# Changing the layout of the S5 branch's input and output by transfers through DRAM instead of products with the identity

## The chip, the cores and the metric

The kernel runs on one core of one Trainium2 chip. A core has a matrix engine (TensorE, PE in the rows below; its weight loads are listed apart as PEld), VectorE (DVE), ScalarE (ACT), GpSimd (POOL) and SyncE (SP), on whose queue nearly all transfers of this kernel are issued, and 16 DMA engines that move the data. Each engine works through its own instructions in order; what one engine needs of another it waits for on semaphores. The metric is the device time of one execution in microseconds (us).

## The reference

The reference is a two-layer encoder over 256 tokens of width 1024. Each layer normalises its input, projects it (`w_in`), runs three mixers side by side (an mLSTM, a Fourier mixer and an S5 state space), gates and adds them, projects back (`w_out`), and then applies a squared-ReLU MLP. The change concerns the S5 mixer, which works on 256 channels as 16 groups of 16:

```python
u = z_s.reshape(bsz, s, S5_GROUPS, S5_GROUP)
bu_re = einsum('gpc,bsgc->bsgp', bb_re, u)          # and bu_im
_, _, x_re, x_im = lax.associative_scan(combine, (a_re, a_im, bu_re, bu_im), axis=1, reverse=reverse)
y = d_skip * u + s5_direction(u, ..., False) + s5_direction(u, ..., True)
y = jax.nn.gelu(y).reshape(bsz, s, M_S5)
zz = y @ w_glu + b_glu
return zz[..., :D_MODEL] * jax.nn.sigmoid(zz[..., D_MODEL:])
```

## The kernel before

Every large product is computed in split precision. A weight block of 512 KB is loaded into one of five buffers `raw` (L200, on SP's queue), ScalarE rounds it to `whi` (L202), VectorE subtracts to get the rest `wlo` (L204), and TensorE makes three products per block of 128 by 128 (`mm3`: L262 hi by hi, L263 hi by the low part of the activations, L264 lo by hi). `whi` and `wlo` have four buffers each. `wstat_pair` makes 256 columns of a projection this way: 48 products of 256 columns, two weight blocks.

The mixers' smaller steps are Python generators. While the main stream of projections is written out, `tick` lets them emit a few instructions after each weight block. The order in which the instructions then stand on each engine is set when the kernel is built, by a scheduler that lists an instruction where its own model of times has it ready; on the chip this order is fixed.

The S5 branch needs its input in another layout than the projection delivers. The projection leaves `zsT`, in channel layout: partition is one of 128 channels of a half `k`, and the 256 tokens are stored as `(t j)`, four tokens `t` of each of 64 chunks `j` (ScalarE's two instructions of L1024). The state space works on `U`, in chunk layout: partition is `32 t + c` (four tokens by the 32 channels of a pair of groups `g`), and the free axes are eight pairs `g` by 64 chunks `j`. `s5_inputs` makes this with 32 small products per layer: each multiplies 32 columns of the identity (`ident`) by one `t` of one half, and places 32 channels in 32 other partitions of a PSUM bank, `acc_ps(0)`, which ScalarE copies to SBUF (L725). `s5_branch` then makes the input products with `QT` (L737), rotations and scans on VectorE, and the output products ("y products", L768 to L776, all into one PSUM bank `yp`), and the GELU (L781 to L786), which gives `g_`, still in chunk layout. Another 32 products with the identity (L792) bring it to channel layout in PSUM, and ScalarE and VectorE split it into `yg`, the high and the low part (L797, L798, two instructions each). The gated linear unit, `glu_up`, multiplies `yg` by `w_glu`.

In layer 0, `s5_branch` is emitted with the gate projections (its tables are made during the projections before), and `glu_up` follows soon after it. In layer 1 it starts with the projections after `zsT`, and `glu_up` comes some 80 us after `yg`. The mLSTM's cells run in between on the same engines: scores on TensorE (L916), an exponential on ScalarE (L924), a product on VectorE (L925), and the cell's value products on TensorE (L933). At the end, `cell_out` transposes the heads (L188), two per head, through PSUM buffers `acc_ps(0)`, of which there are two, and VectorE reads each (L968).

Of the kernel before, what the change touches and what calls it, by code (L numbers as in the profile page):

```python
# [10 lines left out]
F32 = mybir.dt.float32  # L11
F32R = mybir.dt.float32r
AF = mybir.ActivationFunctionType
# [17 lines left out]
NGP = NG // 2  # L31
# [12 lines left out]
LT = 4  # L44
JN = S // LT
# [73 lines left out]
def encoder_kernel(ctx: ExitStack, tc: tile.TileContext, a: dict, out: bass.AP):  # L119
    nc = tc.nc  # L120
# [9 lines left out]
    dp = ctx.enter_context(tc.tile_pool(name="dp", bufs=2, space=DRAM))  # L130
# [3 lines left out]
    def nm(s):  # L134
        uid[0] += 1
        return f"{s}_{uid[0]}"
# [4 lines left out]
    def acc_ps(which):  # L141
        return accp.tile([P, 512], F32, tag=f"acc{which}", name=nm("acc"))

    def ring(which, shape, dt=F32):
        return bp.tile(shape, dt, tag=f"ring{which}", name=nm(f"ring{which}"))
# [13 lines left out]
    act = nc.scalar.activation  # L159
# [3 lines left out]
    mm = nc.tensor.matmul  # L163
# [6 lines left out]
    ident = cst[:, C_ID:C_ID + P]  # L170
# [177 lines left out]
    def w2k():  # L348
        return sp.tile([P, 512], F32, tag="w2k", name=nm("w2k"), bufs=6)
# [366 lines left out]

    def s5_inputs(zsT):

        up = acc_ps(0)
        for g in range(NGP):  # L720
            for tau in range(LT):
                mm(up[32 * tau:32 * tau + 32, g * JN:(g + 1) * JN], ident[:, 32 * (g % 4):32 * (g % 4) + 32],
                   zsT[:, g // 4, tau, :], start=True, stop=True, skip_group_check=True)
        U = cp.tile([P, NGP, JN], F32, tag="zb2", name=nm("U"))
        act(U, up, AF.Copy)  # L725
        return U

    def s5_branch(l, U, yg):
        Z = ring("A", [P, 2, NGP, 2, JN])
        for d in range(2):  # L730
            plus, minus = (ALU.add, ALU.subtract) if d == 0 else (ALU.subtract, ALU.add)
            for b in range(2):
                g0 = d * NGP + 4 * b
                bps = acc_ps(1)
                for g in range(4):
                    for r in range(2):
                        mm(bps[:, (g * 2 + r) * JN:(g * 2 + r + 1) * JN], QT[:, r, g0 + g, :], U[:, 4 * b + g, :],  # L737
                           start=True, stop=True, skip_group_check=True)
                v4 = lambda t: t.rearrange("p (g r j) -> p g r j", g=4, r=2)
                cb = tabC[:, g0:g0 + 4].unsqueeze(2).broadcast_to([P, 4, 2, JN])  # L740
                sb = tabS[:, g0:g0 + 4].unsqueeze(2).broadcast_to([P, 4, 2, JN])
                zg = Z[:, d, 4 * b:4 * b + 4]
                t1, t2 = v4(w2k()), v4(w2k())
                V.tensor_tensor(t1, v4(bps), cb, ALU.mult)
                V.tensor_tensor(t2, v4(bps), sb, ALU.mult)
                yield 1.2
                V.tensor_tensor(zg[:, :, 0], t1[:, :, 0], t2[:, :, 1], plus)
                V.tensor_tensor(zg[:, :, 1], t1[:, :, 1], t2[:, :, 0], minus)
                for g in range(4):
                    c = l * 2 * NGP + g0 + g  # L750
                    rho = par[:, C_RHO, c:c + 1].broadcast_to([P, JN])
                    for r in range(2):
                        zv = zg[:, g, r, :]
                        if d == 1:
                            zv = zv[:, ::-1]
                        V.tensor_tensor_scan(zv, rho, zv, 0.0, ALU.mult, ALU.add)
                yield 1.8
                t1, t2 = v4(w2k()), v4(w2k())
                V.tensor_tensor(t1, zg, cb, ALU.mult)
                V.tensor_tensor(t2, zg, sb, ALU.mult)  # L760
                yield 1.2
                V.tensor_tensor(zg[:, :, 0], t1[:, :, 0], t2[:, :, 1], minus)
                V.tensor_tensor(zg[:, :, 1], t1[:, :, 1], t2[:, :, 0], plus)
                yield 0.7
        yp = acc_ps(1)
        for g in range(NGP):
            o = g * JN
            mm(yp[:, o:o + JN], Tt[:, g, :], U[:, g, :], start=True, stop=False, skip_group_check=True)  # L768
            for d in range(2):
                for r in range(2):  # L770
                    w = Wt[:, r, d * NGP + g].rearrange("p t c -> p (t c)")
                    if d == 0:
                        mm(yp[:, o + 1:o + JN], w, Z[:, d, g, r, 0:JN - 1], start=False, stop=False,  # L773
                           skip_group_check=True)
                    else:
                        mm(yp[:, o:o + JN - 1], w, Z[:, d, g, r, 1:JN], start=False, stop=r == 1,  # L776
                           skip_group_check=True)
        yield 0.0

        q = w2k()  # L780
        act(q, yp, AF.Square)  # L781
        V.tensor_scalar(q, q, 0.044715, 1.0, ALU.mult, ALU.add)
        V.tensor_tensor(q, yp, q, ALU.mult)
        act(q, q, AF.Tanh, scale=GELU_C)
        g_ = w2k()
        stt(g_, q, 1.0, yp, ALU.add, ALU.mult)  # L786
        yield 1.6
        gp = acc_ps(1)
        for g in range(NGP):
            for t in range(LT):  # L790
                o = ((g // 4) * LT + t) * JN
                mm(gp[32 * (g % 4):32 * (g % 4) + 32, o:o + JN], ident[:, 32 * t:32 * t + 32],  # L792
                   g_[:, g * JN:(g + 1) * JN], start=True, stop=True, skip_group_check=True)
        for ct in range(2):
            src = gp[:, ct * S:(ct + 1) * S].rearrange("p (t j) -> p t j", t=LT)
            tok = lambda t: t.rearrange("p (j t) -> p t j", t=LT)
            act(tok(yg[0][:, ct]), src, AF.Copy, scale=0.5)  # L797
            stt(tok(yg[1][:, ct]), src, 0.5, tok(yg[0][:, ct]).bitcast(F32), ALU.mult, ALU.subtract)  # L798
        yield 0.8
# [186 lines left out]
    def mixer(l, iu, vu, after):  # L986
# [40 lines left out]
        st = {"Gm": ring("B", [P, 8, S])}  # L1027
        fo_y = ring("B", [P, 2, 2, S], F32R)
        U = s5_inputs(zsT)
        if l > 0:  # L1030
            side[1].append(s5_branch(l, U, yg))
# [29 lines left out]
        if l == 0:  # L1061
            side[1].append(s5_branch(l, U, yg))
# [275 lines left out]
```

## Time and profile before

| | us |
|---|---|
| median of 3 runs | 842.99 (841.51 to 843.23) |
| the profiled execution, its own time | 842.77 |
| span of its trace | 841.0 |
| TensorE busy in the span | 822.0 (98%) |
| VectorE busy | 598.3 (71%) |
| ScalarE busy | 473.6 (56%) |
| DMA: moved | 145.80 MB, 173 GB/s in the mean |

The span is what the profiler saw from the first to the last instruction; the execution's own time is 1.77 us longer. Busy times of different engines overlap. A matmul's row in the timeline gives its whole duration, and successive matmuls are pipelined, so TensorE's cost is read from the distance between starts or from the chain of work. A matmul on 32-bit operands that are not rounded stands in the trace as two records, so 32 products with the identity are x64.

### The profile page before, as it was taken

To read this page: it belongs to the slowest core of one execution; us is meant where nothing else is said; L and a number is where in the kernel's file an instruction comes from. 1 tells how busy PE (TensorE), PEld (TensorE's weight loads), DVE (VectorE), ACT (ScalarE), POOL (GpSimd) and SP (SyncE) were. 2 spreads that over 40 slices of the span, in tenths; PEclk is the share of its full clock that TensorE was granted. 3 is DMA by queue.
4 is the path that set the end of the run, shared out by engine and by line. 5 is a ranking of instruction groups with operands and counts; after the bars stand their busy time and mean duration, and the time that the engine had idled before them with its cause. 6 is when DMAs were issued, how large, how long until landed. Compare 5 with 4: busy or idle time off the path is not lost.

```text
span 841.0 us, 15400 instructions
## 1 busy us (share of the span) xinstructions
PE 822.0 (98%) x6081; PEld 760.2 (90%) x6081; DVE 598.3 (71%) x1071; ACT 473.6 (56%) x786; POOL 33.6 (4%) x51
## 2 busy tenths in 40 slices
PE   7999999999989999999999999999999999999996
PEld 5999999999868999999879999999997899999995
DVE  4899889868685577667568798676876855555563
ACT  4669855476464448467654355665855544444451
POOL 1000200010020000000010020000000100000000
PEclk9999999999999999999999999999999999999999
DMA  8765645345845665755836452555556556666651
GB/s 262 224 182 160 215 120 159 116 123 157 271 132 164 187 191 136 240 178 187 270 95 213 139 177 76 151 169 158 176 179 222 177 167 183 192 183 191 186 175 50
DMA packets 116824, 145.80 MB, mean 173 GB/s; under 512 B 17894, under 2 KB 98958, under 8 KB 116496
## 3 DMA queue, kind: packets, MB, share of 16 engines
q1 hardware_dynamic: 116604, 144.56, 56.7%
q8 instruction: 47, 0.77, 0.4%
q10 hardware_dynamic: 148, 0.27, 0.1%
q14 instruction: 25, 0.20, 0.1%
HBM read 143.28 MB, written 1.52 MB: 172 GB/s over the span
## 4 chain that ended last, share of the span: by engine, by line
PE 93%; DVE 2%; ACT 1%; issue 1%; DMA 1%; POOL 1%; SPq 0%; DVEq 0%; POOLq 0%; ACTq 0%
PE mm L262 17%; PE mm L264 17%; PE mm L263 17%; PE acc L263 8%; PE acc L264 8%; PE acc L262 8%; PE mm L279 3%; PE mm L278 3%; PE acc L737 2%; PE mm L295 1%; PE acc L188 1%; PE acc L933 1%; PE mm L281 1%; PE acc L916 1%; PE acc L773 1%
## 5 line engine op out<-in xcount | busy, mean ns | idle before, releaser
L204 DVE TENSOR_TENSOR wlo<-raw,whi 128x1024 fp32r<-128x1024 f32 (+1 forms) x237 | 288.2, 1218 | 157.7 <-ACT whi L202 155.9
L202 ACT ACTIVATE whi<-raw 128x1024 fp32r<-128x1024 f32 (+1 forms) x237 | 248.7, 1051 | 248.6 <-PE mm L263 147.2
L262 PE MATMUL mm<-hT,whi 128*128 128x256 f32 x1024 | 291.3, 284 | 0.0
L264 PE MATMUL mm<-hT,wlo 128*128 128x256 f32 x1024 | 290.7, 284 | 0.0
L263 PE MATMUL mm<-hT,whi 128*128 128x256 f32 x1024 | 290.5, 284 | 0.0
L262 PEld LDWEIGHTS mm<-hT,whi 128*128 128x128 f32 x1024 | 192.7, 188 | 1.7
L263 PEld LDWEIGHTS mm<-hT,whi 128*128 128x128 f32 x1024 | 193.0, 188 | 1.2
L264 PEld LDWEIGHTS mm<-hT,wlo 128*128 128x128 f32 x1024 | 193.2, 189 | 0.3
L263 PE MATMUL acc<-wlo,ringB 128*128 128x512 f32 x280 | 109.3, 391 | 0.7 <-DVE wlo L204 0.7
L264 PE MATMUL acc<-whi,ringB 128*128 128x512 f32 x280 | 108.4, 391 | 0.0
L262 PE MATMUL acc<-whi,ringB 128*128 128x512 f32 x280 | 106.5, 390 | 0.0
L263 PEld LDWEIGHTS acc<-wlo,ringB 128*128 128x128 f32 x280 | 52.6, 188 | 12.1 <-DVE wlo L204 1.9
L264 PEld LDWEIGHTS acc<-whi,ringB 128*128 128x128 f32 x280 | 52.6, 188 | 10.9
L262 PEld LDWEIGHTS acc<-whi,ringB 128*128 128x128 f32 x280 | 52.6, 188 | 10.3
L279 PE MATMUL mm<-whi,hT 128*128 128x512 f32 (+1 forms) x84 | 33.1, 401 | 2.0 <-DVE hT L371 1.8
L278 PE MATMUL mm<-whi,hT 128*128 128x512 f32 (+1 forms) x84 | 32.9, 401 | 0.3 <-ACT hT L370 0.2
L900 DVE SCALAR_TENSOR_TENSOR t1k<-ringB,pc,t1k 128x254 f32<-128x254 f32 (+1 forms) x64 | 31.3, 489 | 0.9
L380 DVE SCALAR_TENSOR_TENSOR w2k<-acc,ringA 128x512 f32<-128x512 f32 x16 | 10.6, 688 | 25.6 <-ACT t1k L378 25.6
L340 POOL TENSOR_SCALAR rs<-ss 128x1 f32<-128x1 f32 x16 | 7.8, 488 | 491.4 <-DVE w2k L380 350.0
L262 PE MATMUL mm<-ringB,whi 128*128 128x256 f32 x96 | 27.3, 286 | 0.0
L263 PE MATMUL mm<-ringB,whi 128*128 128x256 f32 x96 | 27.2, 286 | 0.0
L378 ACT ACTIVATE t1k<-acc 128x512 bf16<-128x512 f32 x16 | 9.5, 595 | 31.4 <-PE acc L264 31.4
(339 smaller groups left out, 1197.9 us busy)
## 6 DMA issues: line engine op xcount, KB each, us to landing
raw<-in_w_ffn_dram SPq DMA_DIRECT2D x128, 512.0 KB
raw<-in_w_in_dram SPq DMA_DIRECT2D x84, 512.0 KB
raw<-in_w_out_dram SPq DMA_DIRECT2D x16, 512.0 KB
raw<-in_w_glu_dram SPq DMA_DIRECT2D x16, 256.0 KB
raw<-in_w_up_mlstm_dram SPq DMA_DIRECT2D x8, 512.0 KB
ringB<-md SPq DMA_DIRECT2D x2, 1024.0 KB
raw<-in_w_up_fourier_dram SPq DMA_DIRECT2D x4, 512.0 KB
raw<-in_w_in_dram SPq DMA_DIRECT2D x4, 408.0 KB
```

Of the source, the lines that this page charges most:

```text
L188: nc.tensor.transpose(o, i, cst[:k, C_ID:C_ID + k])
L202: act(hi, raw, AF.Copy)
L204: latest[0] = V.tensor_sub(lo, raw, hi.bitcast(F32)).ins
L262: mm(o, lhi, rhi, start=start, stop=False)
L263: mm(o, lhi, rlo, start=False, stop=False)
L264: mm(o, llo, rhi, start=False, stop=stop)
L278: mm(o, hhi[:, k, tt], hi, start=k == 0, stop=False)
L279: mm(o, hlo[:, k, tt], hi, start=False, stop=False)
L378: act(junk(), ps[c], AF.Square, accum_out=ss[:, c:c + 1])
L380: stt(f, ps[c], ROOT_D, gpost[:, half(c)], ALU.mult, ALU.mult)
L737: mm(bps[:, (g * 2 + r) * JN:(g * 2 + r + 1) * JN], QT[:, r, g0 + g, :], U[:, 4 * b + g, :], start=True, stop=True, skip_group_check=True)
L900: stt(u[:, lo_:hi_], z[:, lo_ + o:hi_ + o], col(l, "cw", j * 8 + i), u[:, lo_:hi_], ALU.mult, ALU.add)
```

## The change

Both layout changes now go through a scratch tensor in DRAM. On the way in, one transfer writes `zsT` to `zd` (pieces of 256 floats, 1 KB), and four transfers, one for each `t`, read it back to 32 partitions of `U` each (pieces of 64 floats, 256 bytes). On the way out, four transfers write `g_` to `gd` (pieces of 256 bytes), and one reads it back in channel layout to an SBUF tile `gp` (pieces of 1 KB). All ten per layer are issued on SP's queue. The 64 products with the identity per layer and ScalarE's copy to `U` go; the two PSUM tiles go as well; `gp` is now one of the six SBUF tiles `w2k`; and `s5_branch` yields once between the transfers and the reading of `gp`.

```diff
     def s5_inputs(zsT):
 
-        up = acc_ps(0)
-        for g in range(NGP):
-            for tau in range(LT):
-                mm(up[32 * tau:32 * tau + 32, g * JN:(g + 1) * JN], ident[:, 32 * (g % 4):32 * (g % 4) + 32],
-                   zsT[:, g // 4, tau, :], start=True, stop=True, skip_group_check=True)
+        zd = dp.tile([NGP, 32, LT, JN], F32, tag="zd", name=nm("zd"))
+        nc.sync.dma_start(by_channel(zd), zsT.rearrange("p k t j -> p k (t j)"))
         U = cp.tile([P, NGP, JN], F32, tag="zb2", name=nm("U"))
-        act(U, up, AF.Copy)
+        for tau in range(LT):
+            nc.sync.dma_start(U[32 * tau:32 * tau + 32], by_chunk(zd, tau))
         return U
+
+    def by_channel(d):
+
+        return d.rearrange("(k q) c t j -> (q c) k (t j)", k=2)
+
+    def by_chunk(d, tau):
+
+        return d[:, :, tau, :].rearrange("g c j -> c g j")
 
     def s5_branch(l, U, yg):
...
-        gp = acc_ps(1)
-        for g in range(NGP):
-            for t in range(LT):
-                o = ((g // 4) * LT + t) * JN
-                mm(gp[32 * (g % 4):32 * (g % 4) + 32, o:o + JN], ident[:, 32 * t:32 * t + 32],
-                   g_[:, g * JN:(g + 1) * JN], start=True, stop=True, skip_group_check=True)
+        gd = dp.tile([NGP, 32, LT, JN], F32, tag="gd", name=nm("gd"))
+        for t in range(LT):
+            nc.sync.dma_start(by_chunk(gd, t), g_[32 * t:32 * t + 32].rearrange("c (g j) -> c g j", g=NGP))
+        gp = w2k()
+        nc.sync.dma_start(gp.rearrange("p (k n) -> p k n", k=2), by_channel(gd))
+        yield 0.0
         for ct in range(2):
             src = gp[:, ct * S:(ct + 1) * S].rearrange("p (t j) -> p t j", t=LT)
```

From here on the changed kernel's lines stand six higher: L737 becomes L743, L768 L774, L797 and L798 become L803 and L804, L916 L922, L924 L930, L933 L939.

The order moves as follows at three places. First, TensorE in layer 1, where the S5 input is used. `mm_5388` before and `mm_5438` after are the same projection, the second after `zsT`. Before, 33 of its 48 products stand between the end of the input's projection and the products with the identity:

```order
L263 MATMUL mm_5388<-hT_85,whi_5460 128x256
L264 MATMUL mm_5388<-hT_84,wlo_5461 128x256
L722 MATMUL acc_5353<-zsT_5180,cst 32x64 x32
L262 MATMUL mm_5388<-hT_84,whi_5460 128x256
L263 MATMUL mm_5388<-hT_85,whi_5460 128x256
```

In the changed kernel the first reader of `U` is L743, and it stands in the projection after that one:

```order
L262 MATMUL mm_5438<-hT_84,whi_5489 128x256
L263 MATMUL mm_5438<-hT_85,whi_5489 128x256
L743 MATMUL acc_5364<-U_5301,QT 128x64 x8
L743 MATMUL acc_5475<-U_5301,QT 128x64 x8
L264 MATMUL mm_5438<-hT_84,wlo_5490 128x256
```

Between the end of the input's projection and L743 stand 80 products now (48 of the projection before and 32 of this one), 47 more than before stood ahead of L722.

Second, ScalarE in layer 0, around the splitting of the S5 output. Before, `yg` stands after the four exponentials of the mLSTM's next head (L924, into `t1k`):

```order
L924 ACTIVATE t1k_1446<-ringB_734,r_119_918 128x256
L924 ACTIVATE t1k_1449<-gx_973,r_119_918 128x128
L924 ACTIVATE t1k_1452<-gx_974,r_119_918 128x128
L924 ACTIVATE t1k_1455<-ringB_734,r_119_918 128x256
L797 ACTIVATE yg_94<-acc_1948 128x4x64 x2
L202 ACTIVATE whi_2591<-raw_2590 128x1024
```

After, it stands ahead of a weight rounding and of the exponentials of a head:

```order
L202 ACTIVATE whi_2379<-raw_2378 128x1024
L803 ACTIVATE yg_94<-w2k_1925 128x4x64 x2
L202 ACTIVATE whi_2411<-raw_2410 128x1024
L909 ACTIVATE t1k_1336<-t1k_1330 128x256
L930 ACTIVATE t1k_1342<-ringB_734,r_119_890 128x256
L930 ACTIVATE t1k_1345<-gx_945,r_119_890 128x128
L930 ACTIVATE t1k_1348<-gx_946,r_119_890 128x128
L930 ACTIVATE t1k_1351<-ringB_734,r_119_890 128x256
```

The exponentials, and with them the value products of that head on TensorE, now stand behind the wait for `gp`. On TensorE, 138 projection products and one pair of score products (L922) stand between the last y product and the first value product of that head (L939, reading `t1k_1342`), and 28 more ahead of `glu_up`. In layer 1 the same count is 143 products and one score pair.

Third, SP's queue in layer 0, around the transfers of the S5 output. Nothing of the kind stood there before, where these weight loads followed each other:

```order
L200 DMA raw_2494<-in_w_glu_dram 128x2x256 x2
L796 DMA gd_1920<-w2k_1888 32x8x64 x4
L798 DMA w2k_1925<-gd_1920 128x2x256
L200 DMA raw_2536<-in_w_glu_dram 128x2x256 x2
L200 DMA raw_2582<-in_w_in_dram 128x4x256
```

The last quarter of `w_glu` and the next projection's weights now stand behind the write of `gd`, which waits for VectorE, and behind the reading back, which waits for that write.

## Rows read from the trace of the kernel before

**Rows 1.** Busy time of each engine in three stretches with S5 work.

```profile
130.00:180.00 50.00, 50.00 (x456) 49.13 (x455) 41.28 (x91) 25.34 (x47) 0.00 (x0) 1.00 0.43 127
460.00:475.00 15.00, 15.00 (x183) 14.77 (x182) 9.36 (x24) 6.68 (x9) 0.00 (x0) 1.00 0.49 142
475.00:505.00 30.00, 30.00 (x252) 29.68 (x250) 29.79 (x71) 14.50 (x26) 4.53 (x4) 1.00 0.51 159
```

**Rows 2.** The chain that ended last, pieces in order: start, length, what.

```profile
43.88 1.03 PE acc L722 x64
...
168.25 0.45 PE acc L792 x6
...
170.67 2.08 PE acc L792 x56
...
464.41 1.03 PE acc L722 x64
...
517.46 2.34 PE acc L792 x64
519.79 1.06 PE acc L916 x4
```

**Rows 3.** Timeline, PE, layer 1, twelve products apart: start, duration, instruction.

```profile
462.81 0.28 PE L262 MATMUL mm<-hT,whi 128*128 128x256 f32 x1
...
464.13 0.28 PE L264 MATMUL mm<-hT,wlo 128*128 128x256 f32 x1
```

**Rows 4.** Timeline of SP's queue: two writes to DRAM and their reading back.

```profile
88.57 0.34 SPq L698 DMA_DIRECT2D kd<-w2k  x1
92.60 2.08 SPq L701 DMA_DIRECT2D Tt<-kd  x4
...
113.11 0.34 SPq L698 DMA_DIRECT2D kd<-w2k  x1
114.83 1.75 SPq L701 DMA_DIRECT2D Tt<-kd  x4
```

**Rows 5.** Timeline, SP and ACT: one weight load and the engine that awaited it.

```profile
208.91 0.33 SPq L200 DMA_DIRECT2D raw<-in_w_out_dram  x1
...
212.51 1.06 ACT L202 ACTIVATE ringA<-raw 128x1024 fp32r<-128x1024 f32 x1 [0.75 <-DMA raw<-in_w_out_dram]
```

**Rows 6.** Timeline, ACT: the last writer of the S5 input, layer 1.

```profile
461.84 0.71 ACT L1024 ACTIVATE zsT<-mm,pc 128x256 f32<-128x256 f32 x1
```

**Rows 7.** Timeline, PE and DVE: last y products and end of the GELU, both layers.

```profile
157.97 0.61 PE L776 MATMUL acc<-ringA,Wt 128*128 128x63 f32 x4
...
164.77 0.68 DVE L786 SCALAR_TENSOR_TENSOR w2k<-w2k,acc 128x512 f32<-128x512 f32 x1
...
510.32 0.61 PE L776 MATMUL acc<-ringA,Wt 128*128 128x63 f32 x4
...
514.39 0.68 DVE L786 SCALAR_TENSOR_TENSOR w2k<-w2k,acc 128x512 f32<-128x512 f32 x1
```

**Rows 8.** Timeline, ACT: S5 output split, conv's tanh, one exponential, one rounding.

```profile
164.02 0.40 ACT L903 ACTIVATE t1k<-t1k 128x256 f32<-128x256 f32 x1
164.33 0.49 ACT L924 ACTIVATE t1k<-ringB,r 128x256 f32<-128x256 f32 x1
...
172.96 0.62 ACT L797 ACTIVATE yg<-acc 128x256 fp32r<-128x256 f32 x1
...
176.72 1.06 ACT L202 ACTIVATE whi<-raw 128x1024 fp32r<-128x1024 f32 x1 [0.94 <-PE mm L263]
```

**Rows 9.** Timeline, DVE: a weight's low part and a head's PSUM read.

```profile
196.40 1.22 DVE L204 TENSOR_TENSOR wlo<-raw,whi 128x1024 fp32r<-128x1024 f32 x1
197.53 0.41 DVE L968 SCALAR_TENSOR_TENSOR t1k<-oth,acc 128x256 f32<-128x256 f32 x1
```

**Rows 10.** Waits of all engines: who waited for whom, us in total, times, longest.

```profile
ACT whi L202 <- PE mm L263: 147.2, 89, 4.5
...
ACT whi L202 <- DMA raw<-in_w_in_dram: 7.3, 5, 2.2
```

## The prediction

> **What bounds the kernel now.** The first view is the busy time by stretches, for the four places where the layout changes. TensorE is busy in the whole of each stretch shown, 50.00 of 50.00 us, 15.00 of 15.00 and 30.00 of 30.00 [rows 1]; nothing else is, except that VectorE comes to 29.79 of 30.00 in the last of them. Then the chain of work that ended last: the products with the identity stand on it as pieces of their own in both layers [rows 2], so they are paid for in full. Then the waits: ScalarE's rounding of weights waited 147.2 us for TensorE to free a buffer and 7.3 us for loads from `w_in` [rows 10]. Weights are ahead of TensorE, and TensorE sets the pace. Last the timeline, for what a trip through DRAM costs here.
>
> **What is removed.** On the input side the chain has 1.03 us per layer [rows 2]. On the output side it has 2.34 us in layer 1; in layer 0, 62 of the 64 records are shown, 0.45 + 2.08 = 2.53 us, so 64 take about 2.6. Together 1.03 + 1.03 + 2.6 + 2.34 = 7.0 us. No new work goes to TensorE. ScalarE's copy to `U` goes too; ScalarE is busy for 6.68 of 15.00 us there [rows 1], and this is priced at nothing.
>
> **What a trip through DRAM costs.** The trace has no transfer of these shapes, but two writes to DRAM that were read back: the next issue followed the write's by 114.83 - 113.11 = 1.72 us, and by 92.60 - 88.57 = 4.03 us [rows 4]. Four issues in a row take 1.75 us, so the fourth is 1.3 us behind the first. For a load, the nearest rows are a 512 KB load, issued at 208.91, whose reader waited for it until 212.51, that is 3.6 us [rows 5], and below it the 1.72 of a whole small write. In the input's trip one write and four loads follow each other: 1.72 to 4.03, plus 1.3, plus 1.72 to 3.6, in sum 4.7 to 8.9 us. The output's trip is four writes and one load, the same sum. I take the middle, 6.8, since at these places some weight loads are in flight and some are not. Under the lower end I expect nothing, as each trip has two landings in it.
>
> Both rows write pieces of 896 bytes (224 floats of a partition, L697), while `gd` is written in pieces of 256, and the sum takes the one turn of these rows for it. The Trainium skill speaks against that: by "DMA: Bandwidth & Descriptors", section Specifications, transfers under 512 bytes are read, modified and written. No row here shows a write that short, so the trace neither bears it out nor denies it; by that rule the sum would end as the first rival does.
>
> **The input's trip.** In layer 0 `U` is read only when `s5_branch` starts with the gate projections, so it is hidden there. In layer 1, `zsT` is complete at 461.84 + 0.71 = 462.55 [rows 6], and `U` lands at 467.3 to 471.5. Before, the products with the identity began on the chain at 464.41 [rows 2]; L743 stands 47 products further on. Eleven distances between starts take 464.13 - 462.81 = 1.32 us [rows 3], 0.12 each, so TensorE reaches L743 at 464.41 + 5.64 = 470.05. It stands still for 0 to 1.5 us; at the middle (469.4), 0.
>
> **The output's trip, layer 0.** The last y products end at 157.97 + 0.61 = 158.58, and `g_` is ready at 164.77 + 0.68 = 165.45 [rows 7], 6.9 us later. Call the end of the y products T. The trip puts the start of the splitting at T + 11.6 to T + 15.8. `yg` itself is in time for `glu_up`. What is not covered is what stands behind it on ScalarE, in the order shown with the change: two copies of 0.62, a rounding of 1.06, a tanh of 0.40 and an exponential of 0.49 [rows 8], 3.2 us. VectorE waits for the rounding (2.3), makes its low part in 1.22 and then two products of a head's size, of 0.4 each [rows 9], which makes 4.4. With the semaphores the first value product of that head can start some 4.5 us after the splitting starts: at T + 16.1 to T + 20.3. TensorE arrives after 138 products and a score pair, 138 times 0.12 plus 1.06 [rows 2], at T + 17.6. It stands for 0 to 2.7 us; at the middle 0.6.
>
> **The output's trip, layer 1.** `g_` is ready 515.07 - 510.93 = 4.1 us after the y products [rows 7], the head's products can start at T + 13.3 to T + 17.5, and TensorE comes after 143 products and a pair, T + 18.2. Nothing is lost even at the slow end. `glu_up` is far off.
>
> **What is queued behind.** In layer 0 SP waits for `g_` and for the write, and the last quarter of `w_glu` and the next weights stand behind it. They are issued at T + 12.2 at the latest; TensorE reads them after 28 more products and three quarters of `glu_up` (72), at T + 17.6 + 12.0 = T + 29.6. A load, a rounding and a low part take 3.6 + 1.06 + 1.22 = 5.9 us [rows 5, 8, 9]. TensorE's products cover the hold by another 11 us, so I price it at nothing; every microsecond beyond that cover would be lost.
>
> **Moved orders.** The scheduler has also moved work that the diff does not touch. The one that can cost: in layer 0 the eight transposes of `cell_out` stand in one row now, and the third head's must wait until VectorE has read the first's PSUM buffer (0.41 us, behind up to one low part of 1.22 [rows 9]). Bounds 0 and 1.6 us; I take 0.7.
>
> **Sum.** Own time 842.77 (0.2 under the median of 842.99): 842.8 - 7.0 + 0 + 0.6 + 0 + 0.7 = 837.1 us. With every wait at its lower bound it is 835.8, with all at their upper bound 842.8 - 7.0 + 1.5 + 2.7 + 1.6 = 841.6. A change within 0.2% (1.7 us) can't be told from none, so "faster" means below 841.3.
>
> **Rivals.**
> - *Short writes cost a second pass.* If each piece of `gd` is read and then written, the write costs one more turn, 1.7 to 4.0 us. Layer 0 pays it all, layer 1 what exceeds its cover of 2.8 us at the middle, 0 to 1.2. That gives 837.1 + 1.7 to 837.1 + 5.2, so 838.8 to 842.3. For it: pieces of 256 bytes; against it: the trace has no such write at all. This is what the Trainium skill's rule would do.
> - *VectorE takes over.* It has 0.2 us to spare in 475 to 505 [rows 1]. If it sets the pace once TensorE is quicker, the 2.06 us of the input side come back as waits: 839.2. Against it: in 460 to 475 it is busy for 9.36 of 15.00, and TensorE has four blocks of weights in front of it.
> - *All waits at their slow ends:* 841.6 and up, no change that can be told. It needs weight loads ahead of every trip, as in the 4.03 us turn.
> - *Slower: the wait for `gp` stops ScalarE.* The splitting holds the roundings and exponentials behind it, in order. If a trip takes x more than 6.8 us, layer 0 loses 0.6 + x, layer 1's output x - 2.8 and its input x - 0.7. Against the 7.0 saved less 0.7, the kernel is 1.7 us slower when 3x - 2.9 reaches 8.0, at x = 3.6, a trip of 10.4 us; at x = 4.5 the time is 847. For it: a turn of 4.03 came behind a 1 MB load, and two weight loads may stand ahead here. Against it: DMA is busy for about half of these stretches (0.43 to 0.51 [rows 1]).
>
> **How the numbers follow.** Forecast 0.50 (835.8 to 839.5), second pass 0.15, VectorE 0.11, no change 0.13, slower 0.11. Below 841.3 lie the forecast, VectorE and most of the second pass: faster 0.74. Within 0.2%: 0.13 plus the rest of the second pass, 0.15. Slower 0.11. The range 835.3 to 842.4 holds the forecast and the first two rivals and most of the third; it leaves out slower and a few per cent on either side.
>
> **What would show it.** Right: no products with the identity, and 128 matmul records fewer on each side. L743's engine idle in layer 1 for under 1 us; the distance from the first `gd` issue to L803's start 5 to 9 us; L939 after `yg` in layer 0 waiting about half a microsecond for VectorE, in layer 1 not at all; ScalarE's rounding still waiting for TensorE, not for loads. A `gd` write turn above 5.3 us would speak for the second pass; TensorE waiting for `wlo` in 475 to 505 for VectorE. I am wrong if TensorE's idle time grows by more than 4 us, or if it does not and the time still is above 841.

## The result, and the profile after

The changed kernel took 834.09 us (median of 4 executions, 832.96 to 836.69) against 843.11 for the kernel before beside it (4 executions): a ratio of 0.990, 95% interval 0.9873 to 0.9927. It is faster, as forecast, but by 9.0 us where 5.7 were forecast, and it lies below the range (835.3 to 842.4). The profiled execution took 834.29 us with a span of 831.6, 9.4 less than the 841.0 before. The experiments below ran the changed kernel six times more, with a median of 835.27, so the first four flattered it somewhat.

Busy time by stretches in the changed kernel, the stretches of [rows 1] moved by what has been saved ahead of them (stretch, length, then PE, PEld, DVE, ACT, POOL busy; granted clock, DMA share, GB/s):

```profile
130.00:180.00 50.00, 50.00 (x420) 49.79 (x420) 42.49 (x95) 29.27 (x58) 0.00 (x0) 1.00 0.51 154
455.00:470.00 15.00, 15.00 (x131) 15.00 (x129) 8.92 (x19) 6.00 (x9) 0.00 (x0) 1.00 0.74 211
470.00:500.00 30.00, 30.00 (x252) 29.61 (x252) 30.00 (x71) 14.39 (x26) 2.71 (x4) 1.00 0.46 142
```

At the places where the layout changes, TensorE is as full as before: the products are gone and no wait has come instead. VectorE is now busy for all of the last stretch and still does not hold TensorE up.

The input's trip in layer 1, in the timelines of SP and PE:

```profile
456.94 0.37 SPq L720 DMA_DIRECT2D zd<-zsT  x1
459.72 1.81 SPq L723 DMA_DIRECT2D U<-zd  x4
464.26 2.00 PE L743 MATMUL acc<-U,QT 128*128 128x64 f32 x17
```

The first reader of `U` follows a projection product without a wait, 7.3 us after the write was issued.

The output's trip, in the timelines of SP, ACT, DVE and PE, layer 0 and then layer 1:

```profile
154.87 1.93 SPq L796 DMA_DIRECT2D gd<-w2k  x4
158.63 0.38 SPq L798 DMA_DIRECT2D w2k<-gd  x1
161.49 1.15 ACT L803 ACTIVATE yg<-w2k 128x256 fp32r<-128x256 f32 x2 [3.35 <-DMA w2k<-gd]
165.15 1.15 DVE L931 SCALAR_TENSOR_TENSOR t1k<-acc,t1k 128x256 f32<-128x256 f32 x4
166.72 0.39 PE L939 MATMUL acc<-v_sb,t1k 128*128 128x129 f32 x2
...
508.43 1.84 SPq L796 DMA_DIRECT2D gd<-w2k  x4
511.85 0.38 SPq L798 DMA_DIRECT2D w2k<-gd  x1
515.86 1.16 ACT L803 ACTIVATE yg<-w2k 128x256 fp32r<-128x256 f32 x2 [2.08 <-DMA w2k<-gd]
```

From the first issue to the splitting it takes 161.49 - 154.87 = 6.6 us and 515.86 - 508.43 = 7.4 (forecast: 4.7 to 8.9, middle 6.8). ScalarE waits for it (3.35 and 2.08), TensorE does not: in layer 0 the head's first value product follows another product without a gap at 166.72, 0.4 us after VectorE was done with its input (165.15 + 1.15). In layer 1 VectorE is done 1.2 us ahead of TensorE.

Where TensorE does stand still, in the timelines of PE, DVE and ACT around the cell transposes of layer 0 (in brackets: the idle time ahead of a row, and what ended it):

```profile
190.07 0.60 PE L188 MATMUL acc<-cst,hm 128*128 128x128 f32 x4
191.30 0.79 PE L188 MATMUL acc<-cst,hm 128*128 128x128 f32 x4 [0.63 <-DVE t1k L974]
193.83 0.39 PE L262 MATMUL mm<-ringB,whi 128*128 128x256 f32 x1 [1.74 <-ACT ringB L976]
...
190.74 0.74 DVE L974 SCALAR_TENSOR_TENSOR t1k<-oth,acc 128x256 f32<-128x256 f32 x2
...
191.62 1.04 ACT L202 ACTIVATE whi<-raw 128x1024 fp32r<-128x1024 f32 x1
192.56 0.81 ACT L1062 ACTIVATE w2k<-mm,pch 128x256 f32<-128x256 f32 x2
193.28 0.90 ACT L976 ACTIVATE ringB<-t1k,pch 128x256 fp32r<-128x256 f32 x2
```

The third head waits 0.63 us for a PSUM buffer, as the prediction had it. Behind the eighth transpose stands one product that reads the heads' output (`ringB`), and it waits 1.74 us more: VectorE has the first head at 191.1 or so, but on ScalarE a rounding and two tanh stand ahead of L976. Together 2.4 us.

And where it stands still less, and faster: around the norm between layer 0's output projection and its MLP. First the stretches with their granted clock, before and then after (columns as above):

```profile
225.00:255.00 30.00, 27.17 (x131) 21.96 (x131) 19.24 (x26) 15.65 (x31) 4.80 (x8) 0.94 0.56 166
425.00:455.00 30.00, 28.33 (x143) 23.53 (x142) 23.53 (x36) 17.15 (x32) 3.67 (x8) 0.94 0.56 179
```

```profile
225.00:255.00 30.00, 27.98 (x139) 22.17 (x139) 23.39 (x30) 18.91 (x34) 4.80 (x8) 1.00 0.59 169
430.00:460.00 30.00, 29.28 (x192) 26.17 (x191) 23.38 (x53) 15.08 (x21) 0.86 (x2) 1.00 0.58 181
```

A mean of 0.94 over 30 us is one stretch of 3.4 us at 0.5, that is 1.2 GHz in place of 2.4, worth at most 1.7 us, where TensorE works all through it. The profile before has two of them, after layer 0's output projection and after layer 0's MLP; the profile after has none there. The timeline of PE ahead of the first, before and then after:

```profile
235.01 0.39 PE L264 MATMUL acc<-ringB,ringB 128*128 128x512 f32 x1
237.55 0.66 PE L188 MATMUL acc<-cst,w2k 128*128 128x128 f32 x4 [2.15 <-DVE w2k L361]
```

```profile
232.76 0.39 PE L264 MATMUL acc<-ringB,ringB 128*128 128x512 f32 x1
234.17 1.10 PE L188 MATMUL acc<-cst,w2k 128*128 128x128 f32 x6 [1.02 <-DVE w2k L361]
```

The norm of the first 128 tokens can start when their last product is done; the products of the other 128 tokens cover it. Before, 17 products of 0.227 us stood behind that last one, in the changed kernel 22: the scheduler moved five of them, which is 5 x 0.227 = 1.1 us less idling (2.15 against 1.02). The diff does not touch this place.

One more difference belongs to the execution alone. Two rows of PE's timeline in the start-up, before and then after:

```profile
16.59 0.63 PE L279 MATMUL mm<-whi,hT 128*128 128x512 f32 x1
...
23.17 0.26 PE L188 MATMUL mm<-cst,w2k 108*128 108x108 f32 x1
```

```profile
16.13 0.39 PE L279 MATMUL mm<-whi,hT 128*128 128x512 f32 x1
...
22.10 0.26 PE L188 MATMUL mm<-cst,w2k 108*128 108x108 f32 x1
```

The same product takes 0.63 us before and 0.39 after, since the clock had already risen there, and the transpose comes 1.1 us earlier. The work ahead of it is the same, and of the other kernels below some started like the one and some like the other.

The sum over the two profiled executions is read from how much earlier the same projection products start in the changed kernel. By the end of layer 0's gates it is 2.25 us: 1.1 from the start-up, less 2.4 at the transposes and less a new wait of 0.25 for `QT` (L685), which leaves 3.8 for the removed products. The norm behind the output projection adds 2.6, that is 1.1 for the five products and 1.5 for the stretch at half clock. The place behind the MLP adds only 0.8 for the other stretch; TensorE's waits there, before and then after, show why:

```profile
440.74 0.63 PE L278 MATMUL mm<-whi,hT 128*128 128x272 f32 x2 [0.25 <-ACT hT L370]
```

```profile
432.80 0.50 PE L278 MATMUL mm<-whi,hT 128*128 128x512 f32 x1 [0.49 <-ACT whi L202]
```

At full clock TensorE comes to a weight that is not rounded yet. Of the fourteen profiles of all runs, this wait (0.46 to 0.49 us) stands in the ten in which the clock did not fall there, one of them a run of the kernel before in another order, and in none of the four in which it did. Layer 1 adds 1.2 at the input and 2.5 at the output (1.03 and 2.34 in the prediction). In sum 9.4, as much as the spans differ by. The removed products are worth 3.8 + 1.2 + 2.5 = 7.5 us in this pair, and the two stretches 2.3. Last the waits that answer to [rows 10]:

```profile
ACT whi L202 <- PE mm L263: 141.6, 86, 6.3
...
ACT whi L202 <- DMA raw<-in_w_in_dram: 7.8, 6, 3.1
...
ACT yg L803 <- DMA w2k<-gd: 5.4, 2, 3.3
```

### The profile page after: what moved, and what is told of

Read it like the earlier page. It is cut to its first block, busy times and chain, and to the rows that moved or that the text cites. A ratio compares the mean times of both kernels' runs of the same rounds, so it can differ in the third digit from the quotient of the medians.

```text
span 831.6 us, 14910 instructions
## 1 busy us (share of the span) xinstructions
PE 810.7 (97%) x5825; PEld 749.4 (90%) x5825; DVE 597.6 (72%) x1071; ACT 472.4 (57%) x784; POOL 30.3 (4%) x51
## 4 chain that ended last, share of the span: by engine, by line
PE 71%; DVE 2%; ACT 1%; issue 1%; POOL 1%; DVEq 0%; POOLq 0%; ACTq 0%
PE mm L262 12%; PE mm L264 12%; PE mm L263 12%; PE acc L263 8%; PE acc L264 8%; PE acc L262 8%; PE mm L279 2%; PE mm L278 2%; PE mm L295 1%; PE mm L188 1%; PE mm L281 1%; PE acc L743 1%; PE acc L939 1%; DVE wlo L204 1%; DVE x_sb L386 0%
## 5 line engine op out<-in xcount | busy, mean ns | idle before, releaser
L279 PE MATMUL mm<-whi,hT 128*128 128x512 f32 (+1 forms) x84 | 30.3, 369 | 1.9 <-DVE hT L371 1.8
L278 PE MATMUL mm<-whi,hT 128*128 128x512 f32 (+1 forms) x84 | 30.5, 373 | 0.7 <-ACT whi L202 0.5
L264 PE MATMUL mm<-ringB,wlo 128*128 128x256 f32 x96 | 27.2, 284 | 0.0
```

What stands on the lines that cost most here:

```text
L264: mm(o, llo, rhi, start=False, stop=stop)
L278: mm(o, hhi[:, k, tt], hi, start=k == 0, stop=False)
L279: mm(o, hlo[:, k, tt], hi, start=False, stop=False)
```

## The experiments

Theory: the removed products give 7.0 us as forecast, the trips cost nothing; the rest of the gain is the moved order of the output projection and the clock, which falls where TensorE stands still. Rival: the clock is luck, and the gain of the trips themselves is larger than the sum. Each kernel's times stand beside the kernel before on the same chip.

**The kernels themselves, run again.** No edit.

> The kernel before, unchanged, run several times. In its profile TensorE's granted clock is at 0.5 for 3.41 us in two places (at about 240 and 434 us), in the changed kernel's profile in neither, and its clock also rose 2.5 us later after the start. Theory 'the clock depends on the execution': mean clocks and spans differ among these executions by whole stretches of 1.7 us (0.002 of the mean clock each), some at 0.996 or 0.998, and some executions come near 840. Rival 'the clock belongs to the kernel': all executions at 0.994 and spans within 0.7 us of 841.0.

> The changed kernel, unchanged, run more often and on the chip of the next three. Theory 'the order of layer 0's output projection spares the clock': mean granted clock mostly 0.998, median 834.1, as in its first runs. Rival 'the first runs were lucky; the standing still at the cell transposes (2.4 us at 190 to 194 us, which in the previous run fell to half clock for 6.83 us) sets off half clock here as well': mean clocks down to 0.99 and a median of 836 to 838.

Measured: before, 841.72 (12 executions), ratio 0.999 (0.9978 to 1.0002) to itself; their mean clocks were 0.994 eight times (spans 839.7 to 840.8), 0.996 three times (838.1 to 838.4) and 0.998 once (837.6). After, 835.27 (6), ratio 0.9929 (0.9908 to 0.995), with mean clocks from 0.992 (835.4) to 0.998 (831.8). So the stretches come and go from execution to execution in both kernels. For the kernel before the theory held; for the changed kernel the result lies between theory and rival: the first four executions were on the lucky side. The profile of this second series has a stretch at half clock at 236.6 us (0.94 over 225 to 255), behind the very norm at which the first profile has none, with the same wait of 1.02.

This needs a way to compare at one clock. Over all 156 executions with a recorded clock (75 of the kernel before), straight lines of one slope, with a level of its own for each kernel, give 0.67 us for each 0.001 of the mean clock; what is left over is 0.7 us for one execution, so that levels from four to six executions are uncertain by 0.3 to 0.4 us. A stretch of 3.4 us takes 0.002 from the mean. The start-up, in which the clock rose at 17.9 us in the profile before and at 15.5 in the one after, is not in this mean.

| kernel | executions | median us | mean clock | level at clock 0.998 |
|---|---|---|---|---|
| before | 75 | 842.2 | 0.9946 | 839.8 |
| before, 22 behind | 6 | 838.6 | 0.9982 | 838.8 |
| before, filled | 12 | 839.8 | 0.9974 | 839.6 |
| input only | 11 | 838.9 | 0.9968 | 838.2 |
| output only | 6 | 836.0 | 0.9968 | 835.3 |
| after | 10 | 834.8 | 0.9959 | 833.7 |
| after, 17 behind | 12 | 840.2 | 0.9919 | 835.4 |
| after, filled | 5 | 834.2 | 0.9970 | 833.6 |
| after, swapped | 5 | 837.1 | 0.9938 | 834.1 |
| after, gates, 22 behind | 4 | 831.2 | 0.9970 | 830.6 |
| the same, 24 behind | 4 | 830.2 | 0.9970 | 829.6 |
| the same as 22, longer trip | 6 | 833.8 | 0.9958 | 832.8 |

At one clock the change is worth 839.8 - 833.7 = 6.1 us.

**Five products moved, in both kernels.** In the kernel before, from 17 to 22:

```diff
                 for k in range(1, NK):
-                    outproj(k, 0)
+                    r = outproj(k, 0)
+                ends.append(r[1][2])
...
+                if l == 0:
+                    for i in (r4[0][1], r4[1][1], r[0][0][0], r[1][0][0]):
+                        behind(i, ends[0])
```

(`behind` fixes the order of two instructions on their engine, without a wait; `r4` and `r` hold the products of the other 128 tokens.) In the changed kernel, back to 17: `for i in (r4[1][2], r[0][0][0]): behind(ends[0], i)`.

> The kernel before, with five products of layer 0's output projection (second half of the tokens) placed behind the last product of the first half instead of ahead of it, as the changed kernel has them; nothing else moves on TensorE. Theory 'order': the five products cover 5 x 0.227 = 1.1 us of the norm that TensorE stood still for (2.15 us before the transposes becomes 1.0): 842.0. Theory 'order, and the clock follows the standing still': with 1.0 us of idling in place of 2.15 the stretch at half clock at 240 us goes too, another 1.7: 840.3. Rival 'neither; the gain of the change is elsewhere': 843.1.

> The changed kernel, with the last product of the first half of the tokens in layer 0's output projection placed behind five products of the second half, as in the kernel before. Theory 'order': 1.1 us more: 835.2. Theory 'order, and the clock follows the standing still': also the stretch at half clock at about 237 us comes back, 1.7: 836.9. Rival 'this order has no part in the gain': 834.1.

Measured: before with 22, 838.57 against 842.62, ratio 0.9959 (0.9943 to 0.9975), mean clock never below 0.996, idling ahead of the transposes 1.02. Five products in another place make the kernel 4.0 us faster without any of the change. After with 17: 840.21, ratio 0.9973 (0.9956 to 0.999), half of its executions at a clock of 0.990. Both runs went past the second theory of each (840.3 and 836.9): the order counts, and the clock's part was larger than the one stretch expected. At one clock the order gives 839.8 - 838.8 = 1.0 and costs 835.4 - 833.7 = 1.7, beside the 1.1 of the rows. With 22 in the kernel before, the stretch behind layer 0's MLP went too, where nothing had been moved; why is open.

In the profile of after with 17, the half clock did not stand where it was expected. The windows around the transposes and around the norm:

```profile
190.00:204.00 14.00, 11.63 (x72) 11.09 (x71) 7.35 (x15) 6.93 (x15) 0.00 (x0) 0.76 0.24 78
225.00:255.00 30.00, 27.23 (x138) 22.00 (x137) 19.62 (x27) 16.32 (x31) 4.79 (x8) 1.00 0.57 168
```

Here 2.15 us of standing still at the norm passed at full clock, and the 2.4 us at the transposes were followed by 6.8 us at half (0.76 over 14 us). A place where TensorE stands still can be followed by it, and is not each time.

**Filling the wait with useless products.** Before, ahead of the norm's transposes, and after, behind the cell transposes (six, `hhi` in place of `mix[0]`):

```diff
+                if l == 0:
+                    junk_ps = mm_ps()
+                    with tc.issue_after(r[1][-1][2].ins):
+                        for i in range(8):
+                            mm(junk_ps, mix[0][:, 0, 0:P], mix[0][:, 0:2, :].rearrange("p k s -> p (k s)"),
+                               start=True, stop=True, skip_group_check=True)
```

> The kernel before, with eight extra products (128x512, 0.23 us each, result unused) on TensorE in the 2.15 us in which it stands still ahead of layer 0's MLP; the transposes that end this wait start when they did. Theory 'the clock follows the standing still': no stretch at half clock at 240 us, 1.7 us less: 841.4. Rival 'the half clock has another cause or is chance': 843.1, and the stretch is still there.

> The changed kernel, with six extra products (128x512, 0.23 us each, result unused) on TensorE behind layer 0's cell transposes, where it stands still for 1.74 us until ScalarE has written the first head; nothing else moves. Theory 'the clock follows the standing still': the stretches at half clock that other runs showed at 193 to 195 us go, mean clock at 0.996 to 0.998 in nearly all executions, the standing still itself stays: 833 to 834. Rival 'this wait has no part in the clock': 834.8, mean clocks from 0.992 to 0.998 as before.

Measured: before, filled, 839.76, ratio 0.9971 (0.996 to 0.9982). The timeline of PE shows the eight products in the wait, and the rest of the wait behind them:

```profile
234.44 1.98 PE L1180 MATMUL mm<-ringB 128*128 128x512 f32 x8
236.76 1.32 PE L188 MATMUL acc<-cst,w2k 128*128 128x128 f32 x8 [0.34 <-DVE w2k L364]
```

The windows of the same execution, around this place and around the norm after the MLP:

```profile
225.00:255.00 30.00, 29.03 (x146) 23.44 (x145) 20.93 (x28) 17.43 (x33) 4.80 (x8) 1.00 0.56 161
420.00:450.00 30.00, 28.34 (x142) 23.53 (x141) 22.67 (x32) 17.39 (x33) 3.66 (x8) 0.94 0.49 151
```

The filled place runs at full clock, the other still fell. Eight products more, and the kernel is 2.9 us faster, with a mean clock of 0.9974 in place of 0.9946; at one clock it stands within 0.2 us of the kernel before. So this gain is the clock's. Read at the same products, the filled place gives 1.4 us between the two profiles, and the start-up another 0.8. In seven of the twelve executions the mean clock is 0.998 or more, so that both stretches were gone, though only one place was filled. The Trainium skill, page "TensorE: Matmul & The Clock Gate", section "Part 1: The HAM clock gate (the "warmup" mystery)", says that the lower clock is TensorE's state at rest and that its activity lifts it; this run agrees, with 1.00 over 225 to 255 where the kernel before has 0.94.

After, filled at the transposes: 834.22, ratio 0.990 (0.988 to 0.992), clocks 0.994 to 0.999, against 834.8 and 0.992 to 0.998. The wait for the first head shrank from 1.74 to 0.3 us. Five executions do not tell this from no effect.

**One half of the change at a time.** Input only: `gp = acc_ps(1)` and the 32 products of the output put back. Output only: `up = acc_ps(0)`, its 32 products and the copy put back.

> Only the S5's input goes through DRAM; its output keeps the products with the identity. The order on TensorE moves again: 22 products stand behind the first half's last one, as in the changed kernel. Sum of rows, against the kernel before with that order (838.6): the two times 1.03 us of products less, no wait: 836.5. Rival 'the input's trip costs a wait': 838 or more. Rival 'the gain is the order's alone': 838.6.

> Only the S5's output goes through DRAM; its input keeps the products. Here 20 products stand behind the first half's last one, and six of the eight cell transposes of layer 0 are spread among projection products. Sum of rows, against the kernel before with 22 (838.6): 2.6 + 2.34 = 4.9 us less, 2 x 0.23 = 0.45 more, nothing lost at the transposes: 834.1, more by whole stretches where the clock falls. Rival 'the output's trip costs TensorE a wait of 1 to 3 us in layer 0': 835 to 837.

Measured: input only 838.93, ratio 0.9968 (0.9955 to 0.9982); output only 835.98, 0.9932 (0.9913 to 0.995). They missed their sums by 2.4 and 1.9 us; 0.9 of each is a lower clock than in the kernel that the sums start from (0.9968 against 0.9982), the rest mostly other waits. With the input only, TensorE stands still for 0.52 + 0.68 = 1.2 us at layer 0's transposes, which the scheduler has placed again:

```profile
194.20 0.41 PE L188 MATMUL acc<-cst,hm 128*128 128x128 f32 x2 [0.52 <-ACT whi L202]
195.28 0.39 PE L262 MATMUL mm<-ringB,whi 128*128 128x256 f32 x1 [0.68 <-ACT ringB L976]
```

Against 838.8 (before, 22 behind) the rows give -2.06 + 1.2 + 0.25 (the wait for `QT`) = -0.6, and at one clock it is -0.6. With the output only they give -4.9 + 0.45 + 0.24 (a wait for `yg` in layer 0) + 0.51 (one for VectorE at 246.7) = -3.7, and it is -3.5. Both times fall where a rival stood (838 or more, 835 to 837), and the profiles decide against it: no reader of `U` waits, and the output's trip costs 0.24 and not 1 to 3. That the input's half is more than the order alone (838.6) rests on those 0.6 us at one clock. Against the kernel before the halves are worth 1.6 and 4.5 us at one clock, in sum 6.1. That this is as much as the whole is chance: both halves have the moved order's gain, and neither has the 2.4 of the transposes.

**The transposes.** The fourth gate projection of layer 0 is written ahead of the mLSTM's output products, and the 22 are held as above; then 24, in both layers:

```diff
-                if len(gates) < 4:
+                while len(gates) < (4 if l == 0 else min(4, 3 + n2)):
                     gates.append(own_gate(len(gates)))
...
-                if l == 0:
-                    for i in (r4[0][1], r4[1][1], r[0][0][0], r[1][0][0]):
-                        behind(i, ends[0])
+                for i in (r4[0][0], r4[1][0], r[0][0][0], r[1][0][0]):
+                    behind(i, ends[0])
```

> The changed kernel, with layer 0's fourth gate projection written ahead of the mLSTM's output products, so that products of it stand between and behind the cell transposes, and with 22 products held behind the first half's last one. Theory 'the transposes cost 2.4 us, and nothing else of the change costs anything': 834.1 - 2.4 = 831.7, which is also the kernel before with 22 products (838.6) less 7.0, 831.6. Rival 'another wait takes the place of this one (gate weights, or VectorE)': 833 to 834.

> The previous version with the fourth gate projection ahead of the mLSTM's output products, and with 24 products in place of 22 behind the first half's last one, in both layers. Theory 'order': 2 x 0.227 = 0.45 us less standing still in each layer, 1.02 becomes 0.57: 831.2 - 0.9 = 830.3, and a mean clock of 0.998. Rival 'these two products hold a weight buffer that the MLP's first weights need': the wait moves behind the norm and the time stays at 831.2.

Measured: 831.24, ratio 0.9874 (0.9855 to 0.9894), and with 24 830.21, ratio 0.9863 (0.9843 to 0.9883): the fastest of all. Stretch of the transposes with 22, and the norms of both layers with 24:

```profile
185.00:200.00 15.00, 15.00 (x128) 15.00 (x127) 12.77 (x22) 11.55 (x23) 3.04 (x2) 1.00 0.59 168
```

```profile
231.24 0.99 PE L188 MATMUL acc<-cst,w2k 128*128 128x128 f32 x5 [0.56 <-DVE w2k L364]
...
636.65 1.32 PE L188 MATMUL acc<-cst,w2k 128*128 128x128 f32 x8 [0.57 <-DVE w2k L364]
```

The 2.4 us of waiting are gone and none took their place. 838.57 - 831.24 = 7.3 us between two kernels with the same 22 products and spread transposes is the most direct measure of the change itself. Their clocks differ somewhat (0.9982 and 0.9970), and the two ran on different chips: at one clock it is 8.2, between the two profiled spans, neither with a stretch at half clock, 836.6 - 828.7 = 7.9, and with each set against the kernel before beside it 10.3 - 4.05 = 6.3. So it is 6 to 8 us, which holds the removed products with trips that cost nothing to be seen.

**The trips.** First the short pieces on the reading side:

```diff
-        gd = dp.tile([NGP, 32, LT, JN], F32, tag="gd", name=nm("gd"))
-        for t in range(LT):
-            nc.sync.dma_start(by_chunk(gd, t), g_[32 * t:32 * t + 32].rearrange("c (g j) -> c g j", g=NGP))
+        gd = dp.tile([P, NGP, JN], F32, tag="gd", name=nm("gd"))
+        nc.sync.dma_start(gd, g_.rearrange("p (g j) -> p g j", g=NGP))
...
+        for q in range(4):
+            nc.sync.dma_start(gp[32 * q:32 * q + 32].rearrange("c (k t j) -> c k t j", k=2, t=LT),
+                              gd.rearrange("(t c) (k q) j -> q c k t j", t=LT, k=2)[q])
```

> The changed kernel, with the S5's output written to DRAM in pieces of 2 KB by one transfer, and read back in pieces of 256 bytes by four: the short pieces are on the reading side. In the changed kernel the splitting starts 6.6 us (layer 0) and 7.4 us (layer 1) after the write is issued, and the reading is issued 3.8 and 3.4 us after it. Theory 'a short write costs no second pass': write turns of 2.3 to 4 us here too, trips of 6 to 8 us. Rival 'a short write is read, modified and written': the write turn falls by half, to under 2 us, and the trip by 1.7 to 4 us. The time is 834 to 836 by both, since TensorE waits for neither trip.

```profile
156.12 0.34 SPq L795 DMA_DIRECT2D gd<-w2k  x1
159.56 2.65 SPq L798 DMA_DIRECT2D w2k<-gd  x4
...
164.00 1.17 ACT L804 ACTIVATE yg<-w2k 128x256 fp32r<-128x256 f32 x2 [0.89 <-DMA w2k<-gd]
```

Measured: write turns of 3.4 us in layer 0 and 2.0 in layer 1 in pieces of 2 KB, against 3.8 and 3.4 in pieces of 256 bytes, in which the four issues alone take 1.9; trips of 7.9 and 7.1 against 6.6 and 7.4. From the end of the last issue to the reading's it is 3.1 and 1.7 us in long pieces, 1.8 and 1.6 in short ones, so no second pass is seen; layer 1's turn fell by 1.4, no more than four issues take longer than one. The Trainium skill's rule on short transfers ("DMA: Bandwidth & Descriptors", section Specifications), which stood as a rival, shows in no run here at this size. The time, 837.14 (0.9942, 0.9925 to 0.996), was above the expected 834 to 836; the clock was 0.9938, and at one clock it is 834.1, as the changed kernel.

Then a hop more, on the version with 22:

```diff
+        ge = dp.tile([NGP, 32, LT, JN], F32, tag="ge", name=nm("ge"))
+        nc.sync.dma_start(ge, gd)
```

> The version with the fourth gate projection moved and 22 products behind the first half (831.2), with the S5's output making one more hop: from one scratch tensor in DRAM to another, before it is read back. In ScalarE's order of layer 0 the splitting now stands behind the tanh and the exponentials of the head that stood behind it. Theory 'what waits for the trip is only what stands behind the splitting': the trip grows by 2 to 4 us, TensorE waits for nothing, 831.2. Rival 'the trips had no room left': in the changed kernel the head's products on VectorE ended 0.4 us ahead of TensorE in layer 0 and 1.2 us in layer 1, so a trip longer by 3 us costs 2.6 + 1.8 = 4.4: 835.6.

Measured: 833.84, ratio 0.9901 (0.9872 to 0.9931), between the two. The trips grew to 9.75 and 10.3 us, by 3.1 and 2.9. In layer 0, with the splitting placed later by the scheduler, nothing on TensorE waits; in layer 1 the head's products wait 0.62 us for VectorE. At one clock the cost is 832.8 - 830.6 = 2.2 us, more than these 0.62. Read at the same products, the two profiles differ by 3.1 us: 0.9 from the start-up, 0.9 at that head in layer 1 and 1.5 at a stretch at half clock behind layer 1's norm, less 0.2 in small pieces. So in this pair the hop costs 0.9; whether the rest of the 2.2 is more than chance, so few executions do not show. In layer 1 the room of the trip was smaller than the 2.9 us that the hop added, as the rows said (1.2).

## Why the prediction was wrong in size

- **What is removed (7.0 us): right, and a little low.** 7.5 us in the sum over the two profiles, 6 to 8 between kernels alike in the rest.
- **The trips: right.** 6.6 and 7.4 us where 6.8 was taken. The output's trip in layer 0 cost 0 in place of 0.6: TensorE came to the head 17.3 us after the y products (17.6 forecast), and its input was ready at 16.9 (16.1 to 20.3). Layer 1's trips cost nothing, as said, nor did SP's held weights. Beside the input's half came a wait of 0.25 us for `QT` in layer 0, which the sum did not have.
- **Moved orders: the term of 0.7 us for the cell transposes was mis-sized; it was 2.4.** The step priced the wait of the third head for a PSUM buffer, 0.63, within its bounds. It did not ask what stands behind the eighth transpose on TensorE. That was a product that reads what ScalarE makes of the first head, 1.74 us away.
- **Moved orders, "the one that can cost": here the step failed.** It looked among the moved orders for those that cost, and missed one that gains: five products behind the first tokens' last one, 1.1 us, countable beforehand on TensorE.
- **The sum: here it failed as well.** It carried the clock of the profile before into the kernel after, as if it were a constant. Two stretches of 3.4 us at half clock stood in the trace of before, worth 2.3 us against the profile after, and its start-up another 1.1. Such stretches hang in part on where TensorE stands still and in part on the execution. At one clock the gain is 6.1 us (rows: 7.5 - 2.4 - 0.25 + 1.1 = 6.0); the forecast of 5.7 comes near that by luck, since its errors cancel: 1.3 us too little for waits (2.4 + 0.25 against 1.3) and 1.6 too little for gains (1.1 for the moved products, 0.5 for the removed ones). The rest of the 9.0 is the clock and four lucky executions. Over all executions the gain is 842.2 - 834.8 = 7.4 us.
- **The rivals.** No second pass; VectorE was full for 30.00 of 30.00 us and did not hold TensorE; no trip stopped the kernel. "TensorE's idle time grows by more than 4 us" did not happen: span less busy time went from 19.0 to 20.9, up at the transposes and down at the norm.

What stays open: which part of the clock's gain belongs to which place in the changed kernel, and why a like wait was followed by half clock in one execution and not in the next. In the fourteen profiles, those of all runs and both kernels, the clock fell behind layer 0's norm in two of three with a wait of 2.15 us and in one of eight with 1.02; at the transposes in two of four with 2.4; behind layer 0's MLP, where the same waits of 0.56 and 0.72 stand in all fourteen, in four. So a shorter wait goes with fewer falls at the norm, and waits alone do not decide.

## What to carry to other kernels

A change in a kernel that a scheduler orders is three changes: the work that is edited, the waits of everything that the scheduler puts elsewhere, and the clock. Before costing the edit, compare the bound engine's order at every place where it stood still before, edited or not, and ask what stands behind a moved group as well as what it waits for. A layout change through DRAM is cheap where, beside what its producer and its readers take, some 7 us of other work stand on the bound engine in both directions; and where TensorE must stand still at a wait, a few products without use can be worth more than they cost (shown at one of the two places tried).

## What the runs showed of the hardware

Two microseconds of standing still on TensorE can be followed by a stretch of 3.4 or 6.8 us at 1.2 GHz, so that the wait is paid for twice; three of seven waits of 2.15 or 2.4 us here passed at full clock. Eight useless products in a wait of 2.15 us made the kernel before 0.29% faster (0.18 to 0.40%). The same kernel's executions differ by up to five microseconds in span (837.3 to 842.4 for the kernel before), and most of that goes with the number of such stretches (mean clock 0.998 to 0.992; 0.7 us is left over). Writing 256 KB to DRAM in pieces of 256 bytes turned around in 3.8 us in layer 0 and 3.4 in layer 1, in pieces of 2 KB in 3.4 and 2.0; the first takes four issues of 1.9 us together, the second one of 0.34, and neither difference is larger than that.
